# Closing scale of a final norm: ScalarE per row and GpSimd per column in place of VectorE

## The chip, the cores and the metric

One core of a Trainium2 chip runs the whole kernel. The metric is the device time of one execution in microseconds; the number to predict is the median over several runs. Three runs of the kernel before gave 2426.24, 2419.15 and 2423.75 us, median 2423.75.

## What is computed

The program is one layer of a hybrid decoder for a prompt of 2048 tokens and a group of 32 sample tokens. Four mixers (convolution, pooling, stick-breaking attention, memory attention) end in one product with `w_out`. What follows that product is where the change lies:

```python
out = rms_norm(mix @ w_out, post_g)     # mix: (tokens, 2048), out: (tokens, 1024)
x = x + out                             # residual
y = rms_norm(x, final_g)                # output
# rms_norm(x, g) = x * rsqrt(mean(x*x, axis=-1) + 1e-6) * g
```

So each output row is multiplied by one number of its own (the row's reciprocal root mean square) and each output column by one number of `final_g`. All arrays are fp32.

## The kernel before

The output is made in 17 tiles: tiles 0 to 15 hold 128 prompt tokens by 1024 columns each, tile 16 holds the 32 sample tokens. The product with `w_out` runs on TensorE as a fast 2 by 2 scheme of seven half-size products, numbered `prod` 1 to 7 in the code, each over eight row blocks `i`. A part (`prod`, `i`, `h`) is half of such a product: four steps over the inner dimension, and in each step three matmuls of 128 columns by 512, because each fp32 operand is split in a high and a low half (`mh` and `ml` for the activations, `wohi` and `wolo` for the weights). ScalarE makes `mh` by a cast (line 1669), VectorE makes `ml` by a subtraction (line 1680). There are four buffers of each, so these two lines can run at most four parts ahead of TensorE. Line 1915 is the matmul.

The program's last 140 us hold products 4, 5 and 3, which finish output tiles: product 5 of block i completes tile 2i + 1, product 3 completes tile 2i. The tiles are completed in the order 1, 3, 5, 0, 2, 4, 16, 7, 6, 9, 8, 11, 10, 13, 12, 15, 14. For each finished accumulator `acc` (a PSUM bank) VectorE adds partial sums kept in SBUF (lines 1723 and 1724, operand `U`), ScalarE squares and row-sums it (1684), VectorE multiplies by `post_g` (1727). For even tiles the left half waits in DRAM and comes back as the SBUF tile `oh`, which GpSimd multiplies by `post_g` (1743). GpSimd also adds two loaded blocks for product 5 (1654, tile `mr`).

`out_tile` then closes the tile. It uses an SBUF tile `oxt` (three buffers), which first receives the residual x by DMA (1749), and a tile `oss` of per-row numbers. `oss` has **one** buffer, so the first write for the next tile (1753) must wait until the last reader of the tile before has read it. The chain for one tile is: 1753 VectorE add of two sums, 1754 ScalarE root, 1755 VectorE reciprocal, 1759 VectorE (two halves) x plus scaled product, 1760 ScalarE (two halves) square and row-sum, 1763 VectorE add, 1764 ScalarE root, 1765 VectorE reciprocal, 1770 VectorE closing scale, 1772 store from the SP queue. The closing scale of tile 15 is held back into the chain of tile 14, which comes last and is closed in two halves.

TensorE's instructions keep the order in which the code issues them. On VectorE, ScalarE, GpSimd and the SP queue a scheduler of the framework places each instruction by its own estimate of when its inputs are there; each engine then runs its list strictly in order. So an edit of one step can move its neighbours on every one of these four.

Of the kernel before, what the change touches and what calls it, by code (L numbers as in the profile page):

```python
# [12 lines left out]
AF = mybir.ActivationFunctionType  # L13
ALU = mybir.AluOpType
# [72 lines left out]
def kernel(  # L87
# [9 lines left out]
    pe, act, dve, pool, sp = nc.tensor, nc.scalar, nc.vector, nc.gpsimd, nc.sync  # L97
# [1647 lines left out]
    def out_tile(t, a, b):  # L1745

        rows = P if t < 16 else NS
        xt = ope.tile([P, D], F32, tag="oxt", name=f"oxt{t}", bufs=OX)[:rows]
        sp.dma_start(xt, xp[P * t : P * t + P, :] if t < 16 else xs)
        if t != 14:  # L1750
            keep["ss"] = ope.tile([P, 6], F32, tag="oss", name=f"oss{t}", bufs=1)
        ss = keep["ss"][:rows, 3:] if t == 14 else keep["ss"][:rows]
        dve.tensor_tensor(out=ss[:, 0:1], in0=ssk[:rows, t, 0:1], in1=ssk[:rows, t, 1:2], op=ALU.add)
        act.activation(out=ss[:, 0:1], in_=ss[:, 0:1], func=AF.Sqrt, bias=eps_t[:rows], scale=1.0 / D)
        dve.reciprocal(out=ss[:, 0:1], in_=ss[:, 0:1])
        last = t == 14
        halves = (slice(0, 512), slice(512, 1024))
        for n, (hs, src) in enumerate(zip(halves, (a[:rows], b[:rows]))):
            dve.scalar_tensor_tensor(out=xt[:, hs], in0=src, scalar=ss[:, 0:1], in1=xt[:, hs], op0=ALU.mult, op1=ALU.add)  # L1759
            act.activation(out=junk[:rows], in_=xt[:, hs], func=AF.Square, accum_out=ss[:, n + 1 : n + 2])  # L1760
        if last:
            keep.pop("end")()
        dve.tensor_tensor(out=ss[:, 1:2], in0=ss[:, 1:2], in1=ss[:, 2:3], op=ALU.add)  # L1763
        act.activation(out=ss[:, 1:2], in_=ss[:, 1:2], func=AF.Sqrt, bias=eps_t[:rows], scale=1.0 / D)  # L1764
        dve.reciprocal(out=ss[:, 1:2], in_=ss[:, 1:2])  # L1765
        dst = y_prompt[0, P * t : P * t + P, :] if t < 16 else y_sample.rearrange("b t d -> (b t) d")

        def end():
            for n, hs in enumerate(halves if last else (slice(0, 1024),)):
                dve.scalar_tensor_tensor(out=xt[:, hs], in0=xt[:, hs], scalar=ss[:, 1:2], in1=gfin[:rows, hs],  # L1770
                                         op0=ALU.mult, op1=ALU.mult)
                (wq if n else sp).dma_start(dst[:, hs], xt[:, hs])

        if t == 15:
            keep["end"] = end
        else:
            end()
# [177 lines left out]
    op = oy.enter_context(tc.tile_pool(name="op", bufs=1, side="right", reuse_waits="tile"))  # L1955
# [74 lines left out]
    for n, x in enumerate(parts):  # L2030
        if n == last_:
# [4 lines left out]
            gfin = ope.tile([P, D], F32, name="gfin", bufs=1)  # L2036
# [58 lines left out]
```

## Time and profile before

| | |
|---|---|
| median of 3 runs | 2423.75 us (2419.15 to 2426.24) |
| time of the profiled execution | 2418.47 us |
| its span, first to last instruction | 2416.7 us |
| TensorE busy | 2285.6 us, 95% |
| VectorE busy | 1718.3 us, 71% |
| ScalarE busy | 1117.5 us, 46% |
| GpSimd busy | 1306.8 us, 54% |

In the rows of the profile PE is TensorE's matmul, PEld its weight load, DVE VectorE, ACT ScalarE, POOL GpSimd, SPq the queue of SyncE that issues the transfers. A row of a group reads: line, engine, operation, output<-inputs, shapes, count, then busy time in us and mean ns of one, then the idle time of that engine just before and what ended it. A row of the timeline reads: start in us, length in us, engine, line, operation, and in square brackets the idle time before it. The shares above are means over very different stages; the change touches only the last 130 us, and there VectorE is far busier than 71%.

### The profile page before, as it was taken

How to read it: one execution, taken by the hardware profiler on the slowest of the kernel's cores; microseconds unless marked ns; L12 is line 12 of the kernel's file. 1: busy time of each engine (PE TensorE's matmuls, PEld its weight loads, DVE VectorE, ACT ScalarE, POOL GpSimd, SP SyncE). 2: the span in 40 equal slices, each digit the busy share in tenths (PEclk: the TensorE clock that was granted, in tenths of full speed). 3: DMA queues.
4: the chain of work that ended last, by engine and by line, in shares of the span. 5: the costliest groups of instructions: out<-in, count | busy, mean ns of one | idle time of the engine just before them, and what ended most of it. 6: DMA issues, size and time to landing. Idle time of an engine off the chain costs nothing. (4 is left out here: it accounts for less than half of the span.)

```text
span 2416.7 us, 42137 instructions
## 1 busy us (share of the span) xinstructions
PE 2285.6 (95%) x15962; PEld 1774.5 (73%) x15962; DVE 1718.3 (71%) x2410; ACT 1117.5 (46%) x1939; POOL 1306.8 (54%) x1333
## 2 busy tenths in 40 slices
PE   7999999999999999999999998899999998989897
PEld 6998978898888777777777776455555556768775
DVE  5333774959757664587877777879798846687998
ACT  5322343242442322124242434788989954443554
POOL 2554544556574555655556564667877755453430
PEclk9999999999999999999999999999999999999998
DMA  5789988887778899987887767834333227887764
GB/s 179 223 260 298 348 290 287 284 272 263 263 254 292 277 344 325 323 287 262 275 270 269 262 218 179 239 79 117 89 88 79 64 64 242 266 272 254 245 234 170
DMA packets 340437, 562.14 MB, mean 233 GB/s; under 512 B 28481, under 2 KB 212929, under 8 KB 323834
## 3 DMA queue, kind: packets, MB, share of 16 engines
q1 hardware_dynamic: 284858, 290.72, 39.2%
q0 software_dynamic: 55376, 268.72, 31.3%
q8 instruction: 126, 2.06, 0.3%
q14 instruction: 77, 0.63, 0.1%
HBM read 469.28 MB, written 90.68 MB: 232 GB/s over the span
## 5 line engine op out<-in xcount | busy, mean ns | idle before, releaser
L959 DVE STREAM_TRANSPOSE T<-kt 128x1024 f32<-128x1024 f32 x256 | 308.9, 1226 | 183.4 <-PE sSA L972 177.2
L926 POOL DMA_INDIRECT vt<-in_cache_v_dram,idv x256 | 251.6, 983 | 242.1 <-PE sO L1011 181.5
L617 DVE SCALAR_TENSOR_TENSOR cacc<-U,par,cacc 128x512 f32<-128x512 f32 x480 | 360.2, 750 | 11.8
L1311 POOL TENSOR_TENSOR be<-be,E 128x512 f32<-128x512 f32 (+2 forms) x320 | 303.8, 957 | 118.4 <-DVE E L1302 52.4
L1302 DVE TENSOR_TENSOR_SCAN E<-gam,cr,ZM 128x513 f32<-128x513 f32 x192 | 232.8, 1262 | 15.1 <-ACT gam L1287 14.2
L926 POOL DMA_INDIRECT kt<-in_cache_k_dram,idk x128 | 126.2, 986 | 201.9 <-DVE T L959 146.8
L1322 PEld LDWEIGHTS AT<-ident,be 128*128 128x128 f32 x1088 | 117.7, 142 | 127.6 <-ACT at L1328 45.4
L1287 ACT ACTIVATE gam<-S,nbias_bc 128x1024 f32<-128x1024 f32 (+1 forms) x160 | 172.6, 1079 | 50.8 <-ACT be L1289 18.9
L1915 PE MATMUL acc<-wohi,mh 128*128 128x512 f32 (+1 forms) x480 | 193.3, 403 | 0.6 <-ACT mh L1669 0.6
L1915 PE MATMUL acc<-wolo,mh 128*128 128x512 f32 (+1 forms) x480 | 189.6, 395 | 0.0
L1915 PE MATMUL acc<-wohi,ml 128*128 128x512 f32 x448 | 178.1, 398 | 11.6 <-DVE ml L1680 11.6
L1282 PE MATMUL S<-kT,Q 128*128 128x512 f32 (+1 forms) x640 | 177.9, 401 | 6.8 <-DMA Q<-qd 2.7
L1289 ACT ACTIVATE be<-S,bias_bc 128x1024 f32<-128x1024 f32 (+1 forms) x160 | 171.6, 1073 | 0.0
L1322 PE MATMUL AT<-ident,be 128*128 128x128 f32 x1088 | 158.1, 284 | 14.1 <-ACT at L1328 4.2
L1338 PE MATMUL av<-at,V 128*64 128x512 f32 (+3 forms) x640 | 153.0, 557 | 1.7 <-DVE sbo L1343 1.7
L972 PE MATMUL sSA<-T,W 128*32 128x128 f32 x4096 | 139.2, 277 | 6.4 <-DVE T L959 5.6
L972 PEld LDWEIGHTS sSA<-T,W 128*32 128x32 f32 x4096 | 104.7, 110 | 43.6 <-issue 35.3
L1680 DVE TENSOR_TENSOR ml<-mr,mh 128x512 fp32r<-128x512 f32 x108 | 98.1, 914 | 38.4 <-ACT mh L1669 38.2
L1282 PEld LDWEIGHTS S<-kT,Q 128*128 128x128 f32 x640 | 107.1, 195 | 23.0 <-ACT be L1289 3.5
L1011 PE MATMUL sO<-vt,saT 128*32 128x512 f32 x1024 | 122.4, 592 | 0.0
L1299 DVE TENSOR_TENSOR_SCAN E<-gam,ZM 128x128 f32<-128x128 f32 (+3 forms) x128 | 96.4, 802 | 30.1 <-ACT gam L1287 25.2
L1328 ACT COPY at<-AT 128x512 f32<-128x512 f32 x192 | 108.9, 655 | 14.4 <-PE AT L1322 14.4
(571 smaller groups left out, 6043.7 us busy)
## 6 DMA issues: line engine op xcount, KB each, us to landing
Q<-qd SPq DMA_DIRECT2D x64, 256.0 KB
mr<-mixd SPq DMA_DIRECT2D x32, 512.0 KB
mr<-mixd SPq DMA_DIRECT2D x48, 256.0 KB
wor<-in_w_out_dram SPq DMA_DIRECT2D x20, 512.0 KB
xtp<-in_x_prompt_dram SPq DMA_DIRECT2D x16, 512.0 KB
kT<-kd SPq DMA_DIRECT2D x64, 128.0 KB
wor<-in_w_out_dram SPq DMA_DIRECT2D x32, 256.0 KB
msd<-mr SPq DMA_DIRECT2D x32, 256.0 KB
```

The lines of the kernel that those rows point to most:

```text
L617: dve.scalar_tensor_tensor(out=ps, in0=U[:, a + k : a + k + H], scalar=wd[:, k : k + 1], in1=ps, op0=ALU.mult, op1=ALU.add)
L926: pool.indirect_dma_start(out=dst, out_offset=None, in_=rows, in_offset=bass.IndirectOffsetOnAxis(ap=idx, axis=0))
L959: dve.transpose(T[:, 2 * hh : 2 * hh + 2].rearrange("p s j t -> p (s j t)"), kt[:, 2 * hh : 2 * hh + 2].rearrange("p s j d -> p (s j d)"))
L972: pe.matmul(sSs[n][32 * g : 32 * g + 32, P * ml : P * (ml + 1)], lhsT=W[:, jj, :], rhs=T[:, :, jj, :], start=i == 0, stop=i == 3, tile_pos ...
L1282: pe.matmul(S[:, j, :w], lhsT=Q[hh][:, x, P * (q2 + j) : P * (q2 + j + 1)], rhs=KT[hp, hh, kc][:, :w], start=x == 0, stop=x == 1)
L1287: act.activation(out=ga[:, :, 512 - w : 512], in_=S[:, :, :w], func=AF.Sigmoid, bias=nbias_bc[:, h : h + 1], scale=-1.0)
L1289: act.activation(out=be[:, :, :w], in_=S[:, :, :w], func=AF.Sigmoid, bias=bias_bc[:, h : h + 1])
L1302: dve.tensor_tensor_scan(out=E[:, j][:, ::-1], data0=ga[:, j][:, ::-1], data1=ZM[:, 0:1].to_broadcast([P, 513]), initial=carry[hh, q2][:, ...
L1311: pool.tensor_tensor(out=be[:, j, :m], in0=be[:, j, :m], in1=E[:, j, 513 - w : 513 - w + m], op=ALU.mult)
L1322: pe.transpose(ap_[:, P * qt : P * (qt + 1)], A[hp, qb, kc, hh, qt][:, P * r : P * (r + 1)], ident)
L1338: pe.matmul(av[64 * hh : 64 * hh + 64, c], lhsT=V[:, 4 * kc + r, 64 * hh : 64 * hh + 64], rhs=ats.pop((hp, qb, kc, r, hh))[:, c], start=dg ...
L1915: pe.matmul(o[:rows], lhsT=m[a][:, k, :rows], rhs=W[prod, 4 * h + k][w], start=not cont and h == k == n == 0, stop=h == 1 and k == 3 and n ...
```

## The change

For tiles 0 to 13 the closing scale, one VectorE instruction of 128x1024, becomes four instructions: for each half of 512 columns ScalarE multiplies `oxt` by the row's number in place, then GpSimd multiplies it by `final_g` (`gfin`) in place. The store waits for the second GpSimd half. Tiles 14, 15 and 16 keep the VectorE instruction.

```diff
         def end():
+            if t < 14:
+                for hs in halves:
+                    act.activation(out=xt[:, hs], in_=xt[:, hs], func=AF.Identity, scale=ss[:, 1:2])
+                    pool.tensor_tensor(out=xt[:, hs], in0=xt[:, hs], in1=gfin[:, hs], op=ALU.mult)
+                sp.dma_start(dst, xt)
+                return
             for n, hs in enumerate(halves if last else (slice(0, 1024),)):
                 dve.scalar_tensor_tensor(out=xt[:, hs], in0=xt[:, hs], scalar=ss[:, 1:2], in1=gfin[:rows, hs],
                                          op0=ALU.mult, op1=ALU.mult)
```

In the kernel after, the new lines are 1771 (ScalarE), 1772 (GpSimd) and 1773 (store), and every line behind them has moved by six: 1770 is 1776.

TensorE's list is the same row for row. The other lists change. The first place is VectorE between the closing of tile 11 and tile 10; `oss_23640` (before) and `oss_23670` (after) belong to tile 11, `oss_23695` and `oss_23728` to tile 10. Before:

```order
L1765 RECIPROCAL oss_23640<-oss_23640 128x1
L1724 TENSOR_TENSOR acc_6_23716<-acc_6_23716,U_20001 128x512
L1770 TENSOR_SCALAR oxt_23638<-oxt_23638,oss_23640,gfin 128x1024
L1680 TENSOR_TENSOR ml_6_1_23771<-mr_6_1_23708,mh_6_1_23770 128x512
L1753 TENSOR_TENSOR oss_23695<-ssk 128x1
L1680 TENSOR_TENSOR ml_7_0_23807<-mr_7_0_23730,mh_7_0_23806 128x512
L1755 RECIPROCAL oss_23695<-oss_23695 128x1
L1759 TENSOR_SCALAR oxt_23693<-oh_5_23562,oss_23695,oxt_23693 128x512
```

After:

```order
L1765 RECIPROCAL oss_23670<-oss_23670 128x1
L1680 TENSOR_TENSOR ml_6_0_23790<-mr_6_0_23704,mh_6_0_23789 128x512
L1753 TENSOR_TENSOR oss_23728<-ssk 128x1
L1755 RECIPROCAL oss_23728<-oss_23728 128x1
L1759 TENSOR_SCALAR oxt_23726<-oh_5_23592,oss_23728,oxt_23726 128x512
L1759 TENSOR_SCALAR oxt_23726<-acc_5_23690,oss_23728,oxt_23726 128x512
L1724 TENSOR_TENSOR acc_6_23752<-acc_6_23752,U_20001 128x512
L1680 TENSOR_TENSOR ml_6_1_23807<-mr_6_1_23744,mh_6_1_23806 128x512
```

The closing scale has left the list, and between tile 11's reciprocal and the first write of `oss` for tile 10 stands one subtraction of 128x512 where before there were a sum, the scale and a subtraction.

The second place is VectorE at the end of the program, from tile 12's reciprocal (`oss_23848` before, `oss_23887` after) to tile 15's first steps (`oss_23942`, `oss_23984`). Before:

```order
L1765 RECIPROCAL oss_23848<-oss_23848 128x1
L1770 TENSOR_SCALAR oxt_23846<-oxt_23846,oss_23848,gfin 128x1024
L1723 TENSOR_TENSOR U_20000<-acc_7_23906,U_20000 128x512
L1724 TENSOR_TENSOR acc_7_23906<-acc_7_23906,U_20001 128x512
L1727 TENSOR_TENSOR acc_7_23906<-acc_7_23906,gpost 128x512
L1753 TENSOR_TENSOR oss_23942<-ssk 128x1
```

After:

```order
L1765 RECIPROCAL oss_23887<-oss_23887 128x1
L1723 TENSOR_TENSOR U_20000<-acc_7_23948,U_20000 128x512
L1724 TENSOR_TENSOR acc_7_23948<-acc_7_23948,U_20001 128x512
L1727 TENSOR_TENSOR acc_7_23948<-acc_7_23948,gpost 128x512
L1753 TENSOR_TENSOR oss_23984<-ssk 128x1
```

Here only the scale is gone, and the rest follows in the order it had.

## The prediction

> **What bounds the kernel now.** I first asked the busy time by stretches of 20 us for the stage that the change touches. The columns are the stretch, its length, then busy us and instructions of PE, PEld, DVE, ACT and POOL, the granted clock, and the share and rate of the transfers:
>
> ```profile
> 2300.00:2320.00 20.00, 18.66 (x79) 12.48 (x78) 17.46 (x29) 8.58 (x27) 7.71 (x5) 1.00 0.71 261
> 2320.00:2340.00 20.00, 18.06 (x78) 14.34 (x79) 18.74 (x33) 11.54 (x31) 7.40 (x4) 1.00 0.69 234
> 2340.00:2360.00 20.00, 20.00 (x89) 16.33 (x88) 18.87 (x36) 11.09 (x31) 5.35 (x4) 1.00 0.67 230
> 2380.00:2400.00 20.00, 19.05 (x83) 15.19 (x82) 17.57 (x34) 10.59 (x30) 1.29 (x1) 1.00 0.52 178
> 2400.00:2417.00 17.00, 0.00 (x0) 0.00 (x0) 9.91 (x21) 5.33 (x16) 0.00 (x0) 0.59 0.23 93
> ```
>
> TensorE and VectorE are both nearly full up to 2400; ScalarE is half idle, GpSimd mostly idle. After 2400 a tail of 17 us has no matmul at all. The timeline of TensorE shows where it stops in this stage, and the timelines of TensorE and VectorE how the tail begins:
>
> ```profile
> 2313.22 0.50 PE L1915 MATMUL acc<-wohi,ml 128*128 128x512 f32 x1 [0.55 <-DVE ml L1680]
> 2319.84 0.50 PE L1915 MATMUL acc<-wohi,ml 128*128 128x512 f32 x1 [0.78 <-DVE ml L1680]
> 2324.83 0.50 PE L1915 MATMUL acc<-wohi,ml 128*128 128x512 f32 x1 [1.94 <-DVE ml L1680]
> 2398.65 0.40 PE L1915 MATMUL acc<-wohi,ml 128*128 128x512 f32 x1
> 2404.96 0.69 DVE L1724 TENSOR_TENSOR acc<-acc,U 128x512 f32<-128x512 f32 x1
> ```
>
> TensorE waits 0.55 + 0.78 + 1.94 = 3.3 us for `ml`, so for VectorE. Its last matmul ends at 2399.05, but VectorE takes up that last accumulator only at 2404.96, 5.9 us late, and everything to the end hangs on that instruction. VectorE therefore sets the end: directly in the tail, and through `ml` before. The most that relieving it can bring is 3.3 + 5.9 = 9.2 us.
>
> **What leaves VectorE.** The groups of the stage from 2277 to 2400 (busy us, mean ns) and, below them, the shortest, median and longest duration of the same lines:
>
> ```profile
> L1680 DVE TENSOR_TENSOR ml<-mr,mh 128x512 fp32r<-128x512 f32 x39 | 30.8, 792 | 1.1 <-ACT mh L1669 1.0
> L1770 DVE SCALAR_TENSOR_TENSOR oxt<-oxt,oss,gfin 128x1024 f32<-128x1024 f32 x14 | 20.6, 1475 | 0.2
> L1753 DVE TENSOR_TENSOR oss<-ssk 128x1 f32<-128x1 f32 x14 | 4.3, 306 | 0.3 <-ACT junk L1684 0.2
> L1763 DVE TENSOR_TENSOR oss<-oss 128x1 f32<-128x1 f32 x14 | 3.3, 234 | 2.1 <-ACT junk L1760 1.8
> L1680 DVE TENSOR_TENSOR mh<-mr,mh 128x128 fp32r<-128x128 f32 x4 | 2.3, 587 | 0.0
> L1654 POOL TENSOR_TENSOR mr<-mr 128x512 f32<-128x512 f32 x10 | 16.4, 1645 | 49.0 <-DVE oss L1765 19.8 <-DMA mr<-mixd 16.9 <-DVE oss L1753 7.1
> L1743 POOL TENSOR_TENSOR oh<-oh,gpost 128x512 f32<-128x512 f32 x8 | 11.2, 1407 | 35.9 <-DVE oss L1765 14.5 <-DMA oh<-c11d 11.2 <-DVE ml L1680 10.0
> ...
> L1680 DVE TENSOR_TENSOR ml<-mr,mh x39: 658/681/1772, 2276.4 to 2394.3; 128x512 fp32r<-128x512 f32 x39
> L1680 DVE TENSOR_TENSOR mh<-mr,mh x4: 271/342/1392, 2300.4 to 2309.7; 128x128 fp32r<-128x128 f32 x4
> L1770 DVE SCALAR_TENSOR_TENSOR oxt<-oxt,oss,gfin x18: 747/1281/2302, 2290.2 to 2412.7; 128x1024 f32<-128x1024 f32 x15, 128x512 f32<-128x512 f32 x2, 32x1024 f32<-32x1024 f32 x1
> L1753 DVE TENSOR_TENSOR oss<-ssk x17: 138/150/1245, 2277.3 to 2407.4; 128x1 f32<-128x1 f32 x16, 32x1 f32<-32x1 f32 x1
> L1763 DVE TENSOR_TENSOR oss<-oss x17: 140/159/1249, 2288.3 to 2411.3; 128x1 f32<-128x1 f32 x16, 32x1 f32<-32x1 f32 x1
> L1743 POOL TENSOR_TENSOR oh<-oh,gpost x8: 1289/1298/1737, 2281.7 to 2384.2; 128x512 f32<-128x512 f32 x8
> ```
>
> The group of line 1770 is exactly the fourteen moved instructions: **20.6 us** leave VectorE.
>
> **What comes back through GpSimd.** The same rows show an odd thing: an addition of one number per row (1753) takes 150 ns in the median and 1245 at most. The timelines of GpSimd and VectorE say when:
>
> ```profile
> 2315.76 1.38 POOL L1654 TENSOR_TENSOR mr<-mr 128x512 f32<-128x512 f32 x1 [1.45 <-DMA mr<-mixd]
> 2315.91 1.25 DVE L1753 TENSOR_TENSOR oss<-ssk 128x1 f32<-128x1 f32 x1
> ...
> 2324.20 3.06 POOL L1654 TENSOR_TENSOR mr<-mr 128x512 f32<-128x512 f32 x1 [7.06 <-DVE oss L1753]
> ...
> 2330.17 1.32 POOL L1743 TENSOR_TENSOR oh<-oh,gpost 128x512 f32<-128x512 f32 x1 [1.05 <-DMA oh<-c11d]
> 2330.45 2.12 DVE L1770 SCALAR_TENSOR_TENSOR oxt<-oxt,oss,gfin 128x1024 f32<-128x1024 f32 x1
> ...
> 2368.36 0.70 DVE L1727 TENSOR_TENSOR acc<-acc,gpost 128x512 f32<-128x512 f32 x1
> 2368.43 1.30 POOL L1743 TENSOR_TENSOR oh<-oh,gpost 128x512 f32<-128x512 f32 x1 [4.25 <-DVE ml L1680]
> 2369.12 0.70 DVE L1727 TENSOR_TENSOR acc<-acc,gpost 128x512 f32<-128x512 f32 x1
> ```
>
> A VectorE instruction with two SBUF inputs that meets a running GpSimd instruction finishes only after it: the tiny 1753 ends at 2317.16, with GpSimd's end at 2317.14. One with an input in PSUM (1727) runs on undisturbed beside it. And GpSimd waits in its turn: 3.06 us for what takes 1.29 alone. The price for VectorE per GpSimd instruction follows from the groups, as busy time over the undisturbed duration (the median, or the shortest for the four small ones): 1680 30.8 - 39 x 0.681 = 4.2, 1770 20.6 - 14 x 1.281 = 2.7, 1753 4.3 - 14 x 0.150 = 2.2, 1763 3.3 - 14 x 0.159 = 1.1, the small 1680 2.3 - 4 x 0.271 = 1.2; together 11.4 us for 10 + 8 = 18 GpSimd instructions, **0.63 us each**. The change adds 28 of the form of line 1743: 28 x 0.63 = **17.6 us**. The bounds are far apart: 0 if each falls beside instructions that read PSUM, as at 2368.43, and 28 x 1.29 = 36 us if each holds VectorE for its whole length, as nearly happened at 2315.76. I take the mean of the rows, because VectorE's list around the new ones holds the same kinds of instruction as around the old.
>
> The Trainium skill, page "SBUF — State Buffer", section "Who interferes with whom", says the same of the inputs and adds that the loser blocks fully; by that rule taken at its worst the sum below would end near +21 us. The page "Perfetto Trace Analysis", section "Optimizing Scalar/DVE Operations", recommends moving work to ScalarE from a saturated VectorE but warns that a move to GpSimd might not help for this reason. The rows above agree with both.
>
> **What comes back through the new wait.** The one `oss` buffer was read last by VectorE itself; now ScalarE's two scalings read it last, and 1753 of the next tile waits for them, with the whole VectorE list queued behind (1755, 1759, and the next `ml`, for which TensorE waits). The trace has no such instruction; nearest is ScalarE's cast of the same shape:
>
> ```profile
> 2338.09 1.12 ACT L1669 CAST mh<-mr 128x512 fp32r<-128x512 f32 x2
> ...
> L1669 ACT CAST mh<-mr 128x512 fp32r<-128x512 f32 x38 | 22.5, 611 | 5.4 <-DMA mr<-msd 3.6 <-issue 1.8
> ```
>
> Two take 1.12 us, with handovers some 1.25. What VectorE has between 1765 and the next 1753 hides it, at about 0.6 us for each instruction of 512 columns. By the new order there is nothing between them for tiles 1 and 5, one such instruction for tiles 0, 4, 9, 11 and 13 (the first place shown above), two or more for the other seven. That makes 2 x 1.25 + 5 x 0.65 = **5.75 us**; if ScalarE is held up by a cast ahead of it, up to 0.6 us more per tile, 8 us. ScalarE itself goes from half busy by 14 x 1.2 = 17 us over 110, which leaves it room.
>
> **What costs nothing, and its cover.** The store leaves later: ScalarE's first half 0.6 and two multiplications 2.6 against 1.28, so about 2 us, up to 4.5 with waits on GpSimd. Behind it in the SP queue stand loads. The load of `oxt` has much slack:
>
> ```profile
> 2381.83 0.33 SPq L1749 DMA_DIRECT2D oxt<-in_x_prompt_dram  x1
> ...
> 2395.14 0.75 DVE L1759 SCALAR_TENSOR_TENSOR oxt<-oh,oss,oxt 128x512 f32<-128x512 f32 x1
> ```
>
> 13.3 us lie between issue and first use. Were that gone, the first 1759 of each tile would move by what is missing. GpSimd's own work for the matmuls (1654) now stands behind multiplications in its list, but its list is under 40% busy in every stretch above.
>
> **The sum.** VectorE: -20.6 + 17.6 + 5.75 = **+2.8 us**. As VectorE sets the end, this goes to the end in full. Against the profiled execution that is 2418.5 + 2.8 = 2421.3 us. That execution lies 5.3 us under the median of the three runs; for the median I add the same difference: 2423.75 + 2.8 = **2426.6 us**. A measurement of this kernel can tell about 0.3%, 7.3 us, from no change.
>
> With x the mean wait per multiplication the sum is 28x - 14.85. It passes +7.3 at x = 0.79 and -7.3 at x = 0.27.
>
> **Rivals.**
>
> *Faster: the multiplications fall beside PSUM work.* If x is below 0.27, VectorE is relieved by more than 7.3 us, TensorE's waits and the lateness at the tail go, and the gain runs to the bound of 9.2 us: 2414.5 us. For it: of the instructions of 512 columns between which the multiplications fall, these groups of the same stage read PSUM and are 62, against 39 subtractions (1680) that don't:
>
> ```profile
> L1727 DVE TENSOR_TENSOR acc<-acc,gpost 128x512 f32<-128x512 f32 x22 | 15.1, 694 | 4.8 <-ACT junk L1684 4.8
> L1759 DVE SCALAR_TENSOR_TENSOR oxt<-acc,oss,oxt 128x512 f32<-128x512 f32 x21 | 15.0, 740 | 0.0
> L1724 DVE TENSOR_TENSOR acc<-acc,U 128x512 f32<-128x512 f32 x19 | 13.0, 685 | 0.0
> ```
>
> Also the last closing, 1.28 us directly ahead of the tail's first instruction, goes for certain (second place). Against it: eighteen GpSimd instructions cost 0.63 each. Chance 0.17.
>
> *Slower: the multiplications strike the chain.* The first multiplication begins when ScalarE has done half a tile, so it is running when 1753 is released, and 1753 has two SBUF inputs; the second then meets 1759 with `oh`, which has two as well, or the next `ml`. If each hit costs 1.0 us on average, the sum is 28 - 14.85 = +13.2 us: 2437 us. It decides from x = 0.79, and shows as TensorE waiting for `ml` later than 2325, where it does not wait now. For it: the first place shows just this sequence, in five of fourteen tiles. Against it: the instruction that is hit was often already waiting for ScalarE, so that wait and hit overlap. Chance 0.38.
>
> *The edit does something else: a table load.* If ScalarE's new function needed another table than the roots, each tile would pay two loads, 28 x 1.28 us by the one load in this stage:
>
> ```profile
> L1754 ACT ACT_TABLE_LOAD x1 | 1.3, 1283 | 0.0
> ```
>
> ScalarE's new list holds no further load, so I give it no chance of its own.
>
> **How the numbers follow.** My forecast, a change within 0.3%, has 0.45; its own range is 2416.5 to 2431. Slower by over 0.3% has 0.38, faster by over 0.3% has 0.17. The range starts at -7.3 us, 2416.5, and reaches to x = 1.1, which is +16 us: 2440. That leaves out most of the faster case and the worst of the slower one, about 2 in 10.
>
> **What would show it.** In the profile of the changed kernel: line 1770's fourteen are gone, 28 scalings of about 0.6 us on ScalarE and 28 multiplications of 1.3 us or more on GpSimd are there; the mean of 1753 rises well over 306 ns; VectorE's idle time ahead of 1753 names ScalarE's closing, about 6 us in all; VectorE takes up the last accumulator about as late after TensorE's end as now, 5.9 us. I am wrong if the excess of the two-SBUF-input instructions over their medians grows by much less than 17 us (then faster), or if TensorE gains new waits for `ml` of more than 3 us in sum after 2325 (then slower), or if a load behind a store ends a wait of VectorE or TensorE.

## The result and the profile after

The changed kernel takes 2426.53 us in the median of ten runs (2424.2 to 2434.16), the kernel before, run beside it, 2419.36 (2417.58 to 2426.24). The medians differ by 7.2 us; the ratio, which goes by the means of the runs and is given with its 95% interval, is **1.0026 [1.0015, 1.0038]**: 6.3 us slower, just inside 0.3%, with an interval that reaches beyond it. The two profiled executions are further apart, 2418.47 and 2426.67 us, spans of 2416.7 and 2425.0. The row of line 1759 with `acc` that stands at the head of the changed stage shows that not all of that is the change's. Before, then after:

```profile
2285.79 1.39 DVE L1759 SCALAR_TENSOR_TENSOR oxt<-acc,oss,oxt 128x512 f32<-128x512 f32 x2
```

```profile
2289.30 1.39 DVE L1759 SCALAR_TENSOR_TENSOR oxt<-acc,oss,oxt 128x512 f32<-128x512 f32 x2
```

Up to this row both run the same instructions, so 3.5 of the 8.3 us of span differ between two executions, not between two kernels. From there to the end it is 2416.7 - 2285.79 = 130.9 us before and 2425.0 - 2289.30 = 135.7 after: **+4.8 us**. I call this the stage, and compare it below. The figure depends a little on the row that it starts from: from the matmul that starts at 2285.86 us before, which is the one at 2290.53 after in TensorE's list, it is +3.6 us. TensorE reaches it 4.7 us later in after and VectorE its row only 3.5.

The busy time of after by stretches, with the columns of the table shown of before:

```profile
2300.00:2320.00 20.00, 17.98 (x78) 12.53 (x78) 13.66 (x29) 13.39 (x36) 8.72 (x7) 1.00 0.67 227
2320.00:2340.00 20.00, 18.92 (x82) 14.85 (x80) 18.09 (x28) 12.56 (x32) 13.89 (x10) 1.00 0.62 205
2340.00:2360.00 20.00, 16.89 (x71) 13.14 (x72) 18.38 (x30) 11.59 (x31) 12.20 (x8) 1.00 0.61 219
2380.00:2400.00 20.00, 19.48 (x86) 15.67 (x85) 18.27 (x30) 14.12 (x35) 11.03 (x8) 1.00 0.55 185
2409.50:2425.00 15.50, 0.00 (x0) 0.00 (x0) 9.02 (x18) 4.90 (x16) 1.66 (x2) 0.56 0.33 130
```

GpSimd has filled up, as it should. VectorE has not emptied: from 2320 on it is about as busy as before, with fewer instructions in each stretch. In the first stretch it is less busy and TensorE is too, which is what waiting looks like. The timelines of TensorE and VectorE show the stops and the last accumulator:

```profile
2316.86 0.45 PE L1921 MATMUL acc<-wohi,mh 128*64 128x512 f32 x1 [2.02 <-DVE mh L1680]
2341.18 0.50 PE L1921 MATMUL acc<-wohi,ml 128*128 128x512 f32 x1 [2.12 <-DVE ml L1680]
2357.49 0.50 PE L1921 MATMUL acc<-wohi,ml 128*128 128x512 f32 x1 [1.32 <-DVE ml L1680]
...
2408.97 0.39 PE L1921 MATMUL acc<-wohi,ml 128*128 128x512 f32 x1
...
2413.17 0.69 DVE L1724 TENSOR_TENSOR acc<-acc,U 128x512 f32<-128x512 f32 x1
```

TensorE now stops at 2341 and 2357, where before it did not stop, and ends 120.1 us into the stage instead of 113.3. VectorE takes up the last accumulator 2413.17 - 2409.36 = 3.8 us late, before it was 5.9. So the loss is made while the matmuls run and shows as a later end of TensorE. The waits from 2275 to 2412, in all, times, longest:

```profile
PE acc L1921 <- DVE ml L1680: 5.5, 6, 2.1
PE acc L1921 <- DVE mh L1680: 2.0, 1, 2.0
DVE oss L1753 <- ACT oxt L1771: 6.2, 9, 1.4
DVE ml L1680 <- ACT mh L1669: 3.1, 9, 1.1
```

And the groups from 2277 to 2407, with one of before, from 2277 to 2400, ahead of them:

```profile
L1759 DVE SCALAR_TENSOR_TENSOR oxt<-oh,oss,oxt 128x512 f32<-128x512 f32 x7 | 5.2, 749 | 0.5
```

```profile
L1680 DVE TENSOR_TENSOR ml<-mr,mh 128x512 fp32r<-128x512 f32 x40 | 32.7, 818 | 3.6 <-ACT mh L1669 3.1
L1763 DVE TENSOR_TENSOR oss<-oss 128x1 f32<-128x1 f32 x14 | 10.4, 746 | 1.8 <-ACT junk L1760 1.8
L1759 DVE SCALAR_TENSOR_TENSOR oxt<-oh,oss,oxt 128x512 f32<-128x512 f32 x7 | 8.2, 1173 | 0.6
L1753 DVE TENSOR_TENSOR oss<-ssk 128x1 f32<-128x1 f32 x14 | 6.6, 470 | 6.1 <-ACT oxt L1771 5.8 <-ACT junk L1684 0.2
L1759 DVE SCALAR_TENSOR_TENSOR oxt<-acc,oss,oxt 128x512 f32<-128x512 f32 x21 | 15.0, 741 | 0.3
L1760 ACT ACTIVATE junk<-oxt 128x512 bf16<-128x512 f32 x28 | 17.7, 631 | 18.8 <-DVE oxt L1759 17.3 <-issue 1.2
L1771 ACT ACTIVATE oxt<-oxt,oss 128x512 f32<-128x512 f32 x26 | 17.4, 716 | 2.0 <-DVE oss L1765 1.5 <-issue 0.4
L1772 POOL TENSOR_TENSOR oxt<-oxt,gfin 128x512 f32<-128x512 f32 x26 | 38.7, 1506 | 19.5 <-ACT oxt L1771 19.5
L1776 DVE SCALAR_TENSOR_TENSOR oxt<-oxt,oss,gfin 32x1024 f32<-32x1024 f32 x1 | 2.3, 2300 | 0.0
L1759 DVE SCALAR_TENSOR_TENSOR oxt<-both,oss,oxt 32x512 f32<-32x512 f32 x1 | 1.2, 1190 | 0.1
L1753 DVE TENSOR_TENSOR oss<-ssk 32x1 f32<-32x1 f32 x1 | 0.8, 848 | 0.3 <-ACT oxt L1771 0.3
L1763 DVE TENSOR_TENSOR oss<-oss 32x1 f32<-32x1 f32 x1 | 0.4, 435 | 0.0
```

An addition of one number per row, 1763, took 234 ns on average and takes 746; 1753 went from 306 to 470; 1759 with `oh`, which has two SBUF inputs, went from 749 to 1173, while 1759 with `acc`, which has one input in PSUM, is unmoved at 741 (740 before). The last four rows are the sample tile's; its closing took 1265 ns before and takes 2300.

Two places show how the two costs arise. First the gap between tile 1 and tile 0, timelines of VectorE, ScalarE and GpSimd of after:

```profile
2293.55 0.15 DVE L1765 RECIPROCAL oss<-oss 128x1 f32<-128x1 f32 x1
2293.74 1.34 ACT L1771 ACTIVATE oxt<-oxt,oss 128x512 f32<-128x512 f32 x2 [0.73 <-DVE oss L1765]
2294.54 2.54 POOL L1772 TENSOR_TENSOR oxt<-oxt,gfin 128x512 f32<-128x512 f32 x2 [6.32 <-ACT oxt L1771]
2295.11 0.74 DVE L1753 TENSOR_TENSOR oss<-ssk 128x1 f32<-128x1 f32 x1 [1.40 <-ACT oxt L1771]
```

VectorE waits 1.40 us for ScalarE's second half, and when it may go on, the first multiplication is under way: the addition ends at 2295.85, at the middle of the pair of multiplications, where the first of them ends. Wait and hit do not overlap here but follow each other: the first half scaled starts the multiplication, and the second half, done while it runs, releases the addition. Second, two hits in a row:

```profile
2364.23 2.98 POOL L1772 TENSOR_TENSOR oxt<-oxt,gfin 128x512 f32<-128x512 f32 x2
...
2364.86 1.21 DVE L1680 TENSOR_TENSOR ml<-mr,mh 128x512 fp32r<-128x512 f32 x1
2365.99 1.23 DVE L1763 TENSOR_TENSOR oss<-oss 128x1 f32<-128x1 f32 x1
```

The second of the two multiplications ends at 2367.21, and 1763 at 2367.22: 1.23 us for an addition that takes 0.16 alone.

### The profile page after: what moved, and what is told of

Read it like the earlier page. It is cut to its first block, busy times and chain, and to the rows that moved or that the text cites. A ratio compares the mean times of both kernels' runs of the same rounds, so it can differ in the third digit from the quotient of the medians.

```text
span 2425.0 us, 42222 instructions
## 1 busy us (share of the span) xinstructions
PE 2288.5 (94%) x15962; PEld 1775.1 (73%) x15962; DVE 1717.3 (71%) x2396; ACT 1135.4 (47%) x1967; POOL 1340.3 (55%) x1361
## 5 line engine op out<-in xcount | busy, mean ns | idle before, releaser
L1322 PEld LDWEIGHTS AT<-ident,be 128*128 128x128 f32 x1088 | 116.4, 141 | 127.3 <-ACT at L1328 45.0
L1287 ACT ACTIVATE gam<-S,nbias_bc 128x1024 f32<-128x1024 f32 (+1 forms) x160 | 172.5, 1078 | 49.6 <-ACT be L1289 18.7
```

Of the source, the lines that this page charges most:

```text
L1287: act.activation(out=ga[:, :, 512 - w : 512], in_=S[:, :, :w], func=AF.Sigmoid, bias=nbias_bc[:, h : h + 1], scale=-1.0)
L1322: pe.transpose(ap_[:, P * qt : P * (qt + 1)], A[hp, qb, kc, hh, qt][:, P * r : P * (r + 1)], ident)
```

## The experiments

Theory A, the prediction's: the 20.6 us come back through hits on VectorE's instructions with two SBUF inputs and through the wait at 1753 for the one `oss`. Rival B: the wait alone. Rival C: ScalarE's 28 scalings, 18.7 us in all, delay the casts. Rival D: the hits are all on the small additions of the chain, and go if these leave VectorE. All ratios are to the kernel before on the same chip, with the 95% interval; 0.1% is 2.4 us. Some runs are also told apart by VectorE's list in the stage, each instruction counted from its start to the next start, with the idle time taken out: 114.0 us of instructions and 13.6 idle before, 111.4 and 20.9 after. One profile stands for each kernel.

**Without the column product.** An edit of after:

```diff
-                    pool.tensor_tensor(out=xt[:, hs], in0=xt[:, hs], in1=gfin[:, hs], op=ALU.mult)
```

> The kernel after without GpSimd's multiplications: tiles 0 to 13 leave the product by final_g out; ScalarE's scalings and the wait for them at 1753 stay. VectorE's list is the same as after's. Theory port: VectorE loses the 20.6 us and gets back only the 6 us of waits and the excess of the 18 old GpSimd instructions; the gain runs to the bound of TensorE's waits and the late tail, 9.2 us: ratio 0.996 to 0.9975, about 2411 us against 2419.4. Theory wait: the multiplications hardly mattered, ratio 1.001 to 1.003. Theory ScalarE (17 us more on ScalarE delay the casts for TensorE): also 1.001 to 1.003.

Measured: 2410.43 us, 0.9965 [0.9951, 0.9979]. Groups from 2275 to 2412:

```profile
L1753 DVE TENSOR_TENSOR oss<-ssk 128x1 f32<-128x1 f32 x15 | 4.9, 329 | 5.2 <-ACT oxt L1771 5.2
L1763 DVE TENSOR_TENSOR oss<-oss 128x1 f32<-128x1 f32 x16 | 4.1, 258 | 3.3 <-ACT junk L1760 3.3
```

1763 is back at 258 ns and the wait at 1753 is still there, 5.2 us, yet the kernel is 8.5 us (0.35%) faster than before. That is nearly the whole bound of 9.2 us, and VectorE takes up the last accumulator at once (0.04 us late). VectorE's list holds 98.9 us of instructions and 20.6 idle: against after only the instructions are shorter, by 12.5 us. By the ratios the multiplications cost about 6.3 + 8.5 = 15 us, and B is out: the wait alone would not have made the change a loss.

**A row number of its own.** In after, the last reciprocal writes to a place that no later tile writes, so that 1753 need not wait for ScalarE:

```diff
-        dve.reciprocal(out=ss[:, 1:2], in_=ss[:, 1:2])
+        rs = ssk[:rows, t, 0:1]
+        dve.reciprocal(out=rs, in_=ss[:, 1:2])
...     # both closings: scale=rs and scalar=rs
```

> The kernel after, with the row's number written to a cell of its own (ssk, per tile) instead of the one oss buffer, so that 1753 of the next tile need not wait for ScalarE's two scalings; the 28 multiplications on GpSimd stay. Against a kernel after that takes 6.3 us more than before (ratio 1.0026). Theory port (VectorE's two-SBUF-input instructions are held up by GpSimd, some 15 us more than before, and the wait at 1753 is the smaller part, 6.2 us): the wait goes, but 1753 is now released while nothing is different for the port; ratio 1.0000 to 1.0015, i.e. 0 to +4 us, and the excess of lines 1680, 1753, 1763 and 1759 with oh stays above 20 us. Theory wait (the new wait and the longer chain are the cost, the port is hidden): the whole loss goes and a good part of the 20.6 us shows, ratio under 0.9975.

Measured: 2417.38 us, 0.9988 [0.9975, 1.0001]. The same place between tiles 1 and 0 in its timelines, and its groups:

```profile
2294.18 0.16 DVE L1766 RECIPROCAL ssk<-oss 128x1 f32<-128x1 f32 x1
2294.37 0.16 DVE L1753 TENSOR_TENSOR oss<-ssk 128x1 f32<-128x1 f32 x1
2295.92 0.16 DVE L1755 RECIPROCAL oss<-oss 128x1 f32<-128x1 f32 x1 [0.79 <-ACT oss L1754]
2295.17 2.54 POOL L1773 TENSOR_TENSOR oxt<-oxt,gfin 128x512 f32<-128x512 f32 x2 [6.92 <-ACT oxt L1772]
```

```profile
L1680 DVE TENSOR_TENSOR ml<-mr,mh 128x512 fp32r<-128x512 f32 x41 | 35.9, 880 | 2.8 <-ACT mh L1669 2.4
L1763 DVE TENSOR_TENSOR oss<-oss 128x1 f32<-128x1 f32 x15 | 8.3, 554 | 1.4 <-ACT junk L1760 1.3
L1753 DVE TENSOR_TENSOR oss<-ssk 128x1 f32<-128x1 f32 x16 | 5.5, 346 | 0.4 <-ACT junk L1684 0.2
L1755 DVE RECIPROCAL oss<-oss 128x1 f32<-128x1 f32 x16 | 2.6, 161 | 7.2 <-ACT oss L1754 7.2
```

The ratio lies between the ranges of the two theories. 1753 no longer waits, and at this place it is through before the multiplication begins: wait and hit went together. But only a part of the waiting is gone. Here ScalarE's pair of scalings starts at 2294.37 and the root (1754) stands behind it, at 2295.61, so that the reciprocal (1755) waits for the root instead: 7.2 us in all, where after has 3.1 in the same window. The stage, from 2289.93 to 2418.8, is 128.9 us, 6.8 shorter than after's. That this is close to the 6.2 us of the wait at 1753 is chance: VectorE's idle time fell by 3.3 us, from 20.9 to 17.6, and its instructions by 3.4, from 111.4 to 108.0. So both terms of A are there, and the one `oss` fed both of them.

**Without the row scaling.** After, without ScalarE's line, the multiplications kept:

```diff
-                    act.activation(out=xt[:, hs], in_=xt[:, hs], func=AF.Identity, scale=ss[:, 1:2])
```

> The kernel after without ScalarE's scalings: tiles 0 to 13 leave the product by the row's number out; GpSimd's 28 multiplications stay and may start as soon as the squares are taken. Nothing waits at 1753 for ScalarE. Theory port: 28 multiplications cost about 0.5 us each as before, the wait of 6.2 us goes, ratio 0.9990 to 1.0010. Theory wait: ratio under 0.9975. Theory ScalarE: clearly under e1, which keeps the scalings, by 3 us or more.

Measured: 2423.27 us, 1.0004 [0.9991, 1.0016]. Its group from 2275 to 2412, as in all that follow:

```profile
L1763 DVE TENSOR_TENSOR oss<-oss 128x1 f32<-128x1 f32 x15 | 14.5, 969 | 1.0 <-ACT junk L1760 1.0
```

ScalarE has 18.7 us less to do, 1753 waits for no scaling, and still it gains less than the kernel with its own row number. VectorE's idle time is back to 13.1 us, about that of before, but its instructions take 117.1 us: the multiplications now start right behind the squares and meet 1763, whose mean rises to 969 ns. The subtractions wait 3.3 us for casts in the stage, where after has 2.8, so C is not seen. What a multiplication costs depends on when it runs.

**The column product on VectorE.** In after, `dve` in place of `pool`:

```diff
-                    pool.tensor_tensor(out=xt[:, hs], in0=xt[:, hs], in1=gfin[:, hs], op=ALU.mult)
+                    dve.tensor_tensor(out=xt[:, hs], in0=xt[:, hs], in1=gfin[:, hs], op=ALU.mult)
```

> The kernel after with the column half on VectorE in place of GpSimd (two multiplications of 128x512): GpSimd does only its 18 old instructions, VectorE keeps about 14 x 1.2 us for the closing, ScalarE scales as after. Theory port: no new port waits, but VectorE's burden is as before and the wait for ScalarE is on top, +6 to +10 us, ratio 1.0025 to 1.0045. Theory wait: the same sign, since the wait is there. If it came out under 1.000, neither the wait nor VectorE's burden would set the end and both theories would fall.

Measured: 2419.33 us, 0.9996 [0.9985, 1.0007], so my expectation of a loss failed.

```profile
L1772 DVE TENSOR_TENSOR oxt<-oxt,gfin 128x512 f32<-128x512 f32 x28 | 21.6, 809 | 1.9 <-ACT oxt L1771 1.8
L1753 DVE TENSOR_TENSOR oss<-ssk 128x1 f32<-128x1 f32 x16 | 2.4, 148 | 0.2 <-ACT junk L1684 0.2
```

I had also said that both theories fall if it comes out under 1.000. It can't be told from 1.000, and the sign was badly set: I had kept the wait at 1753 in that sum. VectorE's own two multiplications now stand ahead of 1753 and fill the time in which ScalarE scales, and no GpSimd instruction strikes it: 148 ns. VectorE does 1 us more work than in the kernel before (21.6 against 20.6) and the time is the same. So the same split closing, kept off GpSimd, costs nothing that these runs can tell.

**One wide multiplication.** In after, one instruction of 1024 columns on each engine:

```diff
-                for hs in halves:
+                for hs in (slice(0, 1024),):
```

> The kernel after with one scaling of 1024 columns on ScalarE and one multiplication of 1024 columns on GpSimd per tile: 14 holds of the port of some 2.5 us in place of 28 of 1.25 us. Theory hold time (a two-input instruction waits for the rest of the hold it meets): a meeting costs twice as much, half as often; the same or up to 5 us more than after, ratio 1.001 to 1.005. Theory count (a fixed price per GpSimd instruction): the port's cost halves, 7 us under after, ratio 0.999 to 1.001.

Measured: 2430.13 us, 1.0050 [1.0037, 1.0063].

```profile
L1680 DVE TENSOR_TENSOR ml<-mr,mh 128x512 fp32r<-128x512 f32 x40 | 39.2, 984 | 2.7 <-ACT mh L1669 2.4
L1772 POOL TENSOR_TENSOR oxt<-oxt,gfin 128x1024 f32<-128x1024 f32 x13 | 31.8, 2446 | 37.1 <-ACT oxt L1771 32.1 <-issue 3.0 <-DMA mr<-mixd 2.0
L1759 DVE SCALAR_TENSOR_TENSOR oxt<-oh,oss,oxt 128x512 f32<-128x512 f32 x7 | 14.5, 2070 | 0.5
```

Half as many instructions, with less time on GpSimd in all (28 x 1.5 = 42 us against 14 x 2.45 = 34), cost more: what they hit waits for a hold of 2.45 us, and 1759 with `oh` takes 2070 ns on average. So the price is not set by the count alone, which I had multiplied with; the length of a hold enters. The edit also doubles ScalarE's scaling, but VectorE's idle time, 20.0 us, is no longer than after's, and its instructions are, 117.6 us against 111.4. The Trainium skill, page "SBUF — State Buffer", section "Who interferes with whom", calls the shared port an exclusive lock; these rows agree.

**The small additions on ScalarE**, in after, alone and with the own row number:

```diff
-        dve.tensor_tensor(out=ss[:, 0:1], in0=ssk[:rows, t, 0:1], in1=ssk[:rows, t, 1:2], op=ALU.add)
+        act.activation(out=ss[:, 0:1], in_=ssk[:rows, t, 0:1], func=AF.Identity, bias=ssk[:rows, t, 1:2])
...
-        dve.tensor_tensor(out=ss[:, 1:2], in0=ss[:, 1:2], in1=ss[:, 2:3], op=ALU.add)
+        act.activation(out=ss[:, 1:2], in_=ss[:, 1:2], func=AF.Identity, bias=ss[:, 2:3])
```

> The kernel after with the two additions of one number per row (1753, 1763) on ScalarE in place of VectorE; oss keeps its one buffer. These are the two-SBUF-input instructions that grew most: 4.5 and 8.2 us over their medians in after. Theory port: VectorE loses their 28 x 0.15 us and their excess of 12.7 us, of which a part moves to the next two-input instruction (1680, 1759 with oh); 6 to 12 us under after, ratio 0.9975 to 1.0000 to before. The wait for the scalings is then ScalarE's own order and costs no hop. Theory wait alone: the wait stays in the chain, which still has to follow the scalings on ScalarE; at most 2 us under after, ratio above 1.0015.

> The kernel after with both: additions on ScalarE and the row's number in a cell of its own. If the port's hits on 1753 and 1763 and the wait at 1753 are two separate costs, both go: ratio 0.995 to 0.997 to before, near the kernel that leaves the multiplications out (0.9965). If they are the same cost counted twice, no better than the own number alone (0.9988).

Measured: 2424.71 us, 1.0008 [0.9995, 1.0022], and with the own number 2424.04 us, 1.0002 [0.9990, 1.0015]. Neither came where it was expected. Groups of the first, then of the second:

```profile
L1680 DVE TENSOR_TENSOR ml<-mr,mh 128x512 fp32r<-128x512 f32 x44 | 42.1, 962 | 7.0 <-ACT mh L1669 6.6
L1759 DVE SCALAR_TENSOR_TENSOR oxt<-oh,oss,oxt 128x512 f32<-128x512 f32 x7 | 9.7, 1385 | 0.6
```

```profile
L1680 DVE TENSOR_TENSOR ml<-mr,mh 128x512 fp32r<-128x512 f32 x43 | 42.4, 989 | 10.5 <-ACT mh L1669 10.3
L1759 DVE SCALAR_TENSOR_TENSOR oxt<-oh,oss,oxt 128x512 f32<-128x512 f32 x7 | 9.4, 1336 | 0.6
```

D falls as it stands and holds in part. With the additions gone the multiplications meet the subtractions (1680: 818 to 962 and 989 ns) and 1759 with `oh` (1173 to 1385 and 1336) instead, and the subtractions now wait for ScalarE's casts as well, 6.6 and 10.3 us. Counted from the last row that the VectorE lists of all these kernels share (a 1724, at 2279.47 in after), with the undisturbed durations of the prediction, 1753 and 1763 lose an excess of 13.3 us, and 1680 and 1759 with `oh` gain 6.2 in the first kernel and 7.3 in the second. So about half of what is taken from the small additions lands on other instructions with two SBUF inputs. From that row to the end the first takes 138.1 us and the second 140.9, where after takes 145.5 and the kernel before 140.9: in these profiles both gain on after, the first by 7.4 us, which is more than by its ratio and as much as was expected.

**The same edits in the kernel before**, closing on VectorE: the additions, the own number, both.

> The kernel before with the same two additions on ScalarE: what they are worth without the change. Both theories: VectorE loses 28 x 0.15 = 4.2 us and an excess of 3.3 us, but ScalarE gains 28 x 0.29 = 8 us; 2 to 6 us faster, ratio 0.9975 to 0.999.

> The kernel before with only the row's number in a cell of its own; closing scale and additions on VectorE. It tells where the gain of before with additions on ScalarE and own number (0.9962) comes from. If the own number pays only where another engine than VectorE writes oss next: ratio 0.9990 to 1.0005 here. If freeing oss lets the scheduler order VectorE's list better by itself: 0.996 to 0.998.

> The kernel before with the additions on ScalarE and the row's number in a cell of its own, the closing scale on VectorE: the control for the one above. The own number brings nothing here, since VectorE is itself the last reader: as the adds alone on before, 0.9975 to 0.999.

Measured: additions 2421.34 us, 0.9993 [0.9982, 1.0004]; own number 2422.06 us, 1.0011 [1.0000, 1.0022]; **both 2415.65 us, 0.9962 [0.9950, 0.9975]** (five runs). None of the three lies in the range that was expected, though the intervals of the first two reach into it. A wait of the first and a group each of the second and the third, from 2275 to 2412:

```profile
ACT oss L1753 <- DVE oxt L1770: 27.0, 15, 3.4
```

```profile
L1771 DVE SCALAR_TENSOR_TENSOR oxt<-oxt,ssk,gfin 128x1024 f32<-128x1024 f32 x15 | 25.1, 1675 | 0.1
```

```profile
L1753 ACT ACTIVATE oss<-ssk 128x1 f32<-128x1 f32 x16 | 4.7, 295 | 1.5 <-DVE ssk L1766 0.5
```

The additions alone put ScalarE in front of the one `oss`, which VectorE's closing frees late: 27.0 us of waiting, and no gain clear of the noise. The own number alone has no such wait to remove, and in its new order the closings are hit harder (1675 ns against 1475). Together the wait is gone, 1.5 us, the small additions have left VectorE, and the last accumulator is taken up 2.2 us late instead of 5.9. This version beats both kernels; by how much is less sure than its interval says, as the table below shows.

**Two tiles only.** The version with both, and the closing moved for tiles 12 and 13 alone, just ahead of the tail:

```diff
+            if t in (12, 13):
+                for hs in halves:
+                    act.activation(out=xt[:, hs], in_=xt[:, hs], func=AF.Identity, scale=rs)
+                    pool.tensor_tensor(out=xt[:, hs], in0=xt[:, hs], in1=gfin[:, hs], op=ALU.mult)
+                sp.dma_start(dst, xt)
+                return
```

> Before with additions on ScalarE and own number (0.9962), with the closing of tiles 12 and 13 alone on ScalarE and GpSimd as in the change. These two stand directly ahead of the tail, where GpSimd has no other work and the wait for oss is gone. VectorE loses 2 x 1.28 us and gets back 4 x 0.5 us: 0 to 2 us under that kernel, ratio 0.9950 to 0.9965. If it came out above 0.9975, even at the best place the move to GpSimd loses.

Measured: 2417.99 us, 0.9998 [0.9985, 1.0010], above the 0.9975 that I had set as the sign that the move loses even here. How much it loses is not settled: by the ratios, which come from two chips, four multiplications cost 8.7 us, but the stage is only 2.1 us longer than in the best version's profile, 129.4 against 127.3.

**After once more**, unchanged, as a yardstick on the chip that also ran the own number in the kernel before, the wide multiplication and the two tiles:

> The kernel after unchanged, as the yardstick of this set: ratio 1.0015 to 1.0038 as measured before.

Measured: 2425.73 us, 1.0022 [1.0011, 1.0034]. The loss is there on a second set of runs, and the stage of its profile is 135.1 us, where the first had 135.7.

The ratios by setting, closing on VectorE against closing moved:

| | on VectorE | moved |
|---|---|---|
| as they are | 1 | 1.0026, again 1.0022 |
| own row number | 1.0011 | 0.9988 |
| additions on ScalarE | 0.9993 | 1.0008 |
| both | 0.9962 | 1.0002 |

The profiles give a second measure. Up to the 1724 named above, at 2275.81 us in before, the lists of VectorE, ScalarE, GpSimd and TensorE are the same in all eight, so what the edits change in these lists comes behind it. From there to the end (us):

| | on VectorE | moved |
|---|---|---|
| as they are | 140.9 | 145.5, again 145.2 |
| own row number | 143.9 | 138.5 |
| additions on ScalarE | 141.0 | 138.1 |
| both | 137.6 | 140.9 |

In the first and the last row the move loses by both measures; in the second, whose ratios come from two chips, it gains by both; in the third the intervals overlap and the profiles have it gain 2.9 us. So the move has no sign of its own. That it hangs on which instruction the order puts beside each multiplication is what the groups above suggest; no run changed that order alone. The two measures part where the ratio says 0.9962, which is -9.2 us, and the profile -3.3, and where the ratio says 1.0008 and the profile -2.8. What differs there lies ahead of the shared row and is not explained, so I do not take the 0.4% of the best version as the size of its gain.

## Why the prediction came out

The forecast was a change within 0.3%, +2.8 us; it is +6.3 [3.6, 9.2], of which the stage shows +4.8. So the direction and the range came true, the size was too small, and whether the change is under 0.3% is not settled by this interval. That 2426.6 us was forecast and 2426.53 measured is luck: the forecast stood on 2423.75 us, the median of three runs of the kernel before, and over ten runs that median is 2419.36. VectorE's list from the stage's first 1759 to its last row gives (us)

| | before | after | change | predicted |
|---|---|---|---|---|
| instructions | 114.0 | 111.4 | -2.6 | -20.6 + 17.6 = -3.0 |
| idle | 13.6 | 20.9 | +7.3 | +5.75 |
| sum | 127.6 | 132.3 | +4.7 | +2.8 |

- **VectorE sets the end: right.** That the list grew by 4.7 us and the stage by 4.8 does not show it, since the list with its idle time runs to the end of the stage in any kernel. What shows it is the kernel without the column product: 12.5 us less of VectorE's instructions than in after, and a gain on before of 8.5 us, near the bound of 9.2, with no lateness left.
- **The port: right in kind, size 15% high.** By the prediction's own working the excess of 1680, 1753, 1763 and the small 1680 was 4.2 + 2.2 + 1.1 + 1.2 = 8.7 us. Now it is 5.5 + 4.5 + 8.2 + 0 on the same rows, with 1680 at 32.7 - 40 x 0.681, 1753 at 6.6 - 14 x 0.150 and 1763 at 10.4 - 14 x 0.159. To that come 3.0 on 1759 with `oh` (8.2 - 7 x 0.749, its mean before) and 2.5 on the four rows of the sample tile (4.8 against 2.3 before): 23.7 us in all, so +15 where 17.6 was said, and 0.54 us for each of the 44 GpSimd instructions of that window instead of 0.63. By this the net of the table should be -5.6; that it is near -3.0 is partly luck: 20.6 us of rows free a little less of the list, since each row overlaps the next by some 0.1 us, 1.4 us for fourteen; where the rest of the difference lies was not traced. The mean of 1753 rose as said, but 1763, which I had not named as a place of hits, was struck harder. The upper bound, 36 us with VectorE held for the whole of each multiplication, was far off.
- **The wait: right in place, too small.** 6.2 us at 1753, naming ScalarE's closing, against 5.75. The term was sized from the cast at 611 ns; the scaling takes 716, a pair 1.34 us instead of 1.12. The rest of the idle time is smaller and of several kinds, which the prediction put at nothing: in the stage 1680 waits 2.8 us for casts instead of 0.7, 1755 waits 2.5 for the root instead of 1.4, and 1727 waits 4.4 for the squares instead of 6.2. That ScalarE had room on average did not keep two casts from standing behind a pair of scalings, at 0.3 us each; the longest wait, 1.1 us at 2303.70, has another cause, named in the last point.
- **"The instruction that is hit was often already waiting, so that wait and hit overlap": wrong.** They add where they were looked at, at 2295.11, and both went there with the own row number. This was my main reason against the slower case. That this is why the result lies on that side of the forecast is not shown: the excess is smaller than forecast, and it is the idle time that is larger.
- **Lateness of the last accumulator, "about as now": wrong.** 3.8 us, not 5.9. The loss went to TensorE's end, through waits for `ml` after 2325 of 5.5 us, past the 3 us that I had named as the sign of the slower case. By that sign I was wrong, and the loss is nearer to the slower case than I had thought; the price of 0.79 us per multiplication from which the case decides was not reached.
- **No price for the store and the table: right in the main.** No wait of VectorE or TensorE ends with a load, and no table load was added. One step further back a load does hold VectorE: ScalarE's cast at 2303.05 waited 1.69 us for a load of `mr`, and the subtraction behind it 1.1 us for the cast, where before such a subtraction did not wait. That load stands behind the store of tile 1, but the store's issue had ended at 2297.45, a subtraction of VectorE ended at 2297.71, and the load left at 2297.78; so the store does not seem to have held it.

## What to carry to other kernels

Before work is moved from VectorE to GpSimd, list VectorE's instructions with two SBUF inputs beside which it will run: here 28 multiplications gave back about 15 of the 20.6 us that left. In this kernel two pieces of 1.3 us for each tile did better than one of 2.45 (1.0022 and 1.0026 against 1.0050). When a closing step moves to another engine, look at how many buffers its operand has: here a number with one buffer turned the move into a wait of the next tile, 6.2 us, and a place of its own took that wait away, though 4.1 us came back one step later, in the wait of 1755. And test such an edit without the move too: in the kernel before, the own number alone was no gain (1.0011).

## What was not expected of the hardware

- A VectorE addition of 128x1, 0.16 us alone, took 0.75 us in the mean and up to 1.25 us beside GpSimd multiplications of 1.3 us, and 1759 with two SBUF inputs took 2.07 us in the mean beside multiplications of 2.45 us.
- ScalarE's multiplication by a number per row took 716 ns for 128x512 fp32 in place, its cast of the same shape 607 to 611, and its square 631.
- Two GpSimd multiplications of 128x512 back to back took 2.54 us at 2294.54; two that met a subtraction and an addition of VectorE took 2.98 us at 2364.23, and the mean of one was 1.51 us. So GpSimd's instructions grow as well.
